# Feed-forward output product as seven products of quarters (Strassen's identity) instead of eight

## The chip, the core and the metric

The kernel runs on one core of a Trainium2 chip. The metric is device time in microseconds from the start of the program to its end, of one launch; lower is better. Before the change it is 849.51 us (median of 3 runs, 849.15 to 849.9). In the text the engines have their names from the profile: PE is TensorE (its matmuls; PEld its weight loads), DVE is VectorE, ACT is ScalarE, POOL is GpSimd, SP is SyncE, which here only issues transfers. SBUF is the on-chip memory of 128 partitions, PSUM the eight banks into which PE writes (128 x 512 float32 each).

## The reference

One layer of a decoder trunk for 512 tokens of 1024 channels, all in float32. The last part is the one that is changed:

```python
hf = rms_norm(x, ffn_norm_g[l]) @ w_ffn_in[l]      # 512x1024 @ 1024x5632
gt, up = jnp.split(hf, 2, axis=-1)                  # 512x2816 each
x = x + (jax.nn.silu(gt) * up) @ w_ffn_out[l]       # 512x2816 @ 2816x1024
```

Ahead of it stand a normed input projection, three branches (an attention without softmax, a convolution of width 31, one of width 3), their gated sum and an output projection; the change doesn't touch them.

## The kernel before, in words

**Precision.** Every float32 operand of a large product is split into two numbers of the type float32r: hi is a cast of the value (ACT, L81), lo the rest (DVE, L82). A product a x b is then three matmuls into the same PSUM bank: a_hi b_hi, a_hi b_lo, a_lo b_hi (mm3, L92 to L95; L90 is the matmul itself). A matmul here has 128 contraction rows, a stationary operand of 128 columns and a moving one of 512.

**Weights.** They come by DMA on SP's queue into one of three buffers `raw` of up to 8 KB a partition (L134), and wsplit turns pieces of up to 1024 columns into a pair `wh`, `wl`, three buffers each. A buffer is loaded or written anew when the last reader of its third predecessor is done, so this ring of three sets how far the transfers and the splits run ahead of PE.

**Order.** PE's instructions stand in the order in which the program writes them. For the other engines a scheduler sets the order when the program is built; the code gives priorities (the loads and splits of weights are high). On the chip each engine works off its row in that order and waits at each instruction for what it needs, so what stands behind a waiting instruction waits too.

**The feed-forward part** runs twice, each time over one half of the 2816 inner channels (11 blocks of 128). ffn_in makes for each block two products of 24 matmuls, gate and up (8 channel blocks x 3 terms, tokens on the moving side), and from them silu(gate) times up, scaled by the reciprocal norm (L759 to L762); the 128 x 512 block h (channels x tokens) is split into hi and lo. Then rows_product makes the output product of this half in two column halves: h is the stationary operand (128 tokens at a time), the weight rows of 512 columns the moving one, and four PSUM banks hold four blocks of 128 tokens. That is 11 x 4 x 3 = 132 matmuls for a column half, 264 for a half of the channels. When a bank is done, DVE adds it to x1, the running sum in SBUF (tiles `v`; L787), and in the second half of the channels into a tile that goes out by DMA from ACT's queue (L790, L791). PSUM tiles: tag mm has four banks, z three, o one.

**POOL** has nothing to do in this part; its last work before it are seven adds for the norm (L717).

Of the kernel before, what the change touches and what calls it, by code (L numbers as in the profile page):

```python
# [14 lines left out]
P = 128  # L15
# [20 lines left out]
def hybrid_layer(ctx, tc, x, mix_norm_g, w_in, q_norm_g, k_norm_g, w_attn_out, conf_dw_w,  # L36
# [19 lines left out]
    BUFS = {"raw": 3, "wh": 3, "wl": 3, "u": 16, "m": 18, "b": 8, "v": 2, "cf": 5, "c": 4, "t": 6,  # L56
            "s": 2, "a": 4, "l0": 2, "r": 2, "l1": 1, "l2": 1, "mm": 4, "z": 3, "o": 1}
    count = [0]
# [684 lines left out]

    half = DFF // P // 2
    later_h = []

    def ffn_in(c, h):
        for j0 in range(0, half, 2):
            n = min(2, half - j0)
            b = (c * half + j0) * P  # L750
            wg, wu = [once(lambda o=o, b=b, n=n: raw(w_ffn_in[:, o + b:o + b + n * P], KT, n * P))
                      for o in (0, DFF)]
            for j in range(n):
                pg = []

                def up(pu, pg=pg):
                    def fn():
                        g, u = tmp(), tmp()
                        nc.vector.tensor_mul(g, pg[0], rstd[0])  # L759
                        act(g, g, AF.Silu)  # L760
                        nc.vector.tensor_mul(u, pu, rstd[0])  # L761
                        nc.vector.tensor_mul(g, g, u)  # L762
                        h.append(split(g, "m" if len(h) < 9 else "b"))
                    if rstd:
# [3 lines left out]

                yield unit(wg, j, lambda: u2, pg.append)
                yield unit(wu, j, lambda: u2, up)  # L770

    for c in range(2):
        h = []
        queue.extend(ffn_in(c, h))
        if c == 0:
# [5 lines left out]
        drain()  # L781
        for n in range(2):
            cs = slice(n * S, (n + 1) * S)

            def add(i, o, n=n, cs=cs, c=c):
                if c == 0:
                    nc.vector.tensor_add(x1[n][:, i, :], o, x1[n][:, i, :])  # L787
                else:
                    y = tmp()
                    nc.vector.tensor_add(y, o, x1[n][:, i, :])  # L790
                    nc.scalar.dma_start(out[i * P:(i + 1) * P, cs], y)  # L791

            queue.append(rows_product(w_ffn_out[c * half * P:(c + 1) * half * P], cs, h, BANKS[n],
                                      add))
            drain()

# [30 lines left out]
```

## Time and profile before

| what | value |
|---|---|
| median of 3 runs | 849.51 us |
| the profiled execution | 849.84 us, its span on the core 848.1 us |
| PE busy | 835.9 us, 99% of the span |
| DVE, ACT, POOL busy | 518.0, 361.8, 35.1 us |
| first half of the output product | 604.9 to 664.8 us |
| second half of the output product | 784.5 to 844.3 us |
| DMA | 81.44 MB, 96 GB/s on average |

A row of the chain of waits gives start, length, engine, tile and line of work that followed without a gap on the way to the end. A row of the groups gives line, engine, operation, output and inputs with shapes, then the number, busy time in all, mean ns of one, and the idle time of the engine ahead of them with what ended it. A row of the timeline gives start and length of one or some instructions in a row. A row of the stretches gives for each engine the busy time and number of instructions (PE, PEld, DVE, ACT, POOL in this order), the granted clock of PE, the DMA engines' share and GB/s. Matmuls overlap, and their ends are modelled, so their pace is read from their starts.

### The profile page before, as it was taken

What the parts mean: (1) busy time and instruction counts of PE and PEld (TensorE: products, weight loads), DVE (VectorE), ACT (ScalarE), POOL (GpSimd) and SP (SyncE); (2) the same over time, 40 slices, a digit from 0 to 9 for tenths busy, and PEclk for the clock granted to TensorE, in tenths of its full rate; (3) what the DMA queues carried; (4) which work ended last, traced back from release to release, by engine and by line L of the source; (5) the groups of instructions that cost most, each with busy time, mean ns of one, the idle gap of its engine ahead of it and who ended that gap; (6) DMA issues with size and microseconds to landing.
All of it is one profiled execution on the core that took longest, in us unless ns stands there. A gap on an engine that the chain in (4) does not pass through costs nothing.

```text
span 848.1 us, 9544 instructions
## 1 busy us (share of the span) xinstructions
PE 835.9 (99%) x3793; PEld 695.6 (82%) x3793; DVE 518.0 (61%) x725; ACT 361.8 (43%) x531; POOL 35.1 (4%) x60
## 2 busy tenths in 40 slices
PE   6999999999999999999999999999999999999998
PEld 6888887888888888888888888888888888888886
DVE  5598799896899999774543455444422544444231
ACT  5436698876664223563342353222221232222120
POOL 2100010002100000000000120000000000000000
PEclk9999999999999999999999999999999999999999
DMA  7333114122112232233253222324224233223311
GB/s 249 103 100 94 56 50 150 50 61 89 50 50 100 73 126 100 71 129 99 100 199 100 64 85 100 100 75 147 72 80 149 100 99 100 75 67 126 102 54 49
DMA packets 73016, 81.44 MB, mean 96 GB/s; under 512 B 1616, under 2 KB 58124, under 8 KB 72972
## 3 DMA queue, kind: packets, MB, share of 16 engines
q1 hardware_dynamic: 71804, 78.74, 28.5%
q10 hardware_dynamic: 1168, 2.10, 0.6%
q8 instruction: 29, 0.48, 0.2%
q14 instruction: 15, 0.12, 0.0%
HBM read 78.74 MB, written 2.10 MB: 95 GB/s over the span
## 4 chain that ended last, share of the span: by engine, by line
PE 95%; DVE 3%; issue 1%; ACT 0%; DMA 0%; SPq 0%; DVEq 0%
PE mm L90 78%; PE z L90 12%; PE o L90 4%; PE mm L296 1%; DVE cf L502 0%; DVE wl L82 0%; DMA m<-in_x_dram 0%; PE z L296 0%; PE mm L705 0%; DVE t L82 0%; DVE m L375 0%; DVE m L376 0%; DVE t L263 0%; DVE s L448 0%; DVE l L82 0%
## 5 line engine op out<-in xcount | busy, mean ns | idle before, releaser
L90 PE MATMUL mm<-u,wh 128*128 128x512 f32 x1536 | 475.1, 390 | 0.0
L90 PEld LDWEIGHTS mm<-u,wh 128*128 128x128 f32 x1536 | 287.4, 188 | 59.4 <-DVE u L710 0.6
L81 ACT CAST wh<-raw 128x1024 fp32r<-128x1024 f32 (+1 forms) x156 | 151.7, 975 | 364.1 <-PE mm L90 260.0
L90 PE MATMUL mm<-u,wl 128*128 128x512 f32 x768 | 299.2, 390 | 0.0
L82 DVE TENSOR_TENSOR wl<-raw,wh 128x1024 fp32r<-128x1024 f32 (+1 forms) x154 | 174.5, 1135 | 122.1 <-ACT wh L81 121.8
L90 PEld LDWEIGHTS mm<-u,wl 128*128 128x128 f32 x768 | 144.2, 188 | 30.0
L502 DVE SCALAR_TENSOR_TENSOR cf<-cf,cols_w,cf 128x512 f32<-128x512 f32 x120 | 89.8, 748 | 3.7 <-ACT cf L500 1.2
L761 DVE TENSOR_TENSOR t<-mm,cf 128x512 f32<-128x512 f32 x22 | 15.2, 691 | 66.8 <-PE mm L90 66.8
L90 PE MATMUL mm<-wh,m 128*128 128x512 f32 x176 | 55.6, 389 | 0.0
L90 PE MATMUL z<-wh,m 128*128 128x512 f32 x132 | 45.2, 392 | 0.0
L759 DVE TENSOR_TENSOR t<-mm,cf 128x512 f32<-128x512 f32 x22 | 15.2, 691 | 42.8 <-PE mm L90 42.8
L90 PE MATMUL mm<-m,wh 128*128 128x512 f32 x128 | 39.4, 389 | 0.0
L90 PEld LDWEIGHTS mm<-wh,m 128*128 128x128 f32 x176 | 33.0, 188 | 6.9
L90 PE MATMUL mm<-wl,m 128*128 128x512 f32 x88 | 34.2, 389 | 0.0
L90 PEld LDWEIGHTS z<-wh,m 128*128 128x128 f32 x132 | 24.8, 188 | 5.1
L90 PEld LDWEIGHTS mm<-m,wh 128*128 128x128 f32 x128 | 24.0, 188 | 4.9
L78 ACT ACTIVATE s<-s 128x384 f32<-128x384 f32 (+1 forms) x48 | 26.9, 560 | 1.1
L90 PE MATMUL z<-wl,m 128*128 128x512 f32 x66 | 25.7, 389 | 0.0
L90 PE MATMUL mm<-m,wl 128*128 128x512 f32 x64 | 24.9, 389 | 0.0
L448 DVE SCALAR_TENSOR_TENSOR s<-z,s 128x384 f32<-128x384 f32 (+1 forms) x24 | 14.4, 598 | 11.6 <-ACT s L78 10.4
L90 PE MATMUL mm<-wh,b 128*128 128x512 f32 x64 | 21.2, 389 | 0.0
L717 POOL TENSOR_TENSOR cf<-cf,t 128x512 f32<-128x512 f32 x7 | 9.9, 1415 | 255.3 <-ACT t L715 255.0
(197 smaller groups left out, 879.9 us busy)
## 6 DMA issues: line engine op xcount, KB each, us to landing
raw<-in_w_in_dram SPq DMA_DIRECT2D x23, 1024.0 KB
raw<-in_w_ffn_in_dram SPq DMA_DIRECT2D x20, 1024.0 KB
raw<-in_w_ffn_out_dram SPq DMA_DIRECT2D x8, 1024.0 KB
raw<-in_w_in_dram SPq DMA_DIRECT2D x10, 512.0 KB
raw<-in_w_o_dram SPq DMA_DIRECT2D x4, 1024.0 KB
raw<-in_w_ffn_out_dram SPq DMA_DIRECT2D x4, 768.0 KB
m<-in_x_dram SPq DMA_DIRECT2D x8, 256.0 KB
raw<-in_w_sc_out_dram SPq DMA_DIRECT2D x2, 1024.0 KB
```

The lines of the kernel that those rows point to most:

```text
L78: table(nc.scalar.activation(o, i, f, **kw))
L81: (copy or nc.scalar.copy)(hi, src)
L82: (sub or nc.vector.tensor_sub)(lo, src, hi.bitcast(F32))
L90: nc.tensor.matmul(o, lhsT, rhs, start=start, stop=stop, skip_group_check=True)
L296: nc.tensor.matmul(pts[f][:, t * P:(t + 1) * P], xblock(xt, t, f), diag, start=True, stop=True, skip_group_check=True)
L448: marks.append(nc.vector.scalar_tensor_tensor(t, z, 0.0, t, ALU.max, ALU.add))
L502: nc.vector.scalar_tensor_tensor(y, pad[:, n:n + S], w(n), y, ALU.mult, ALU.add)
L717: nc.gpsimd.tensor_add(sumsq, sumsq, s)
L759: nc.vector.tensor_mul(g, pg[0], rstd[0])
L761: nc.vector.tensor_mul(u, pu, rstd[0])
```

## The change

The inner channels are taken in two chunks of 12 and 10 blocks instead of 11 and 11, and in pairs of blocks. For a pair, h is a matrix of 2 x 2 quarters A (channel block by half of the tokens, 128 x 256 each) and the weights one of 2 x 2 quarters B (channel block by half of the columns, 128 x 512 each). Instead of eight products of quarters the program makes seven, of sums of quarters (the form of Strassen's identity with 4 + 4 sums ahead and 7 behind; those behind are made on the totals over a chunk, and not for each pair).

- quarters makes four 128 x 256 sums of A per pair on DVE and splits all operands; the operands lie in buffers that earlier parts of the kernel have left (tags m, b, a, l0, l2, s, l1, c).
- ffn_out goes over the pairs twice. Pass 1 makes products 1, 7 and 6 of all pairs (banks p1, p7, p6; 18 matmuls a pair); for it three of the four quarters of weights are loaded, two sums t3, t2 made on DVE (L835, L836) and split. Then p6 and p7 are taken out: ACT copies p1 (L847), DVE adds (L848, L849), POOL makes six adds into x1 (L850 to L852), and p1 goes on in its banks. Pass 2 loads all four quarters, makes t1 and t4 (L863 to L865) and products 2, 3, 4 and 5 (24 matmuls a pair; in the last pair in reverse), 2 into the banks of p1.
- After pass 2, ten adds (L876) bring p5, p4, p3 and p1 into x1, and in the last chunk out.

```diff
@@ -54,7 +54,7 @@
     cst = pool("cst", bufs=1)
     ps = pool("ps", bufs=1, space=PSUM)
     BUFS = {"raw": 3, "wh": 3, "wl": 3, "u": 16, "m": 18, "b": 8, "v": 2, "cf": 5, "c": 4, "t": 6,
-            "s": 2, "a": 4, "l0": 2, "r": 2, "l1": 1, "l2": 1, "mm": 4, "z": 3, "o": 1}
+            "s": 2, "a": 4, "l0": 2, "r": 2, "l1": 1, "l2": 1, "tt": 2, "mm": 4, "z": 3, "o": 1}
     count = [0]
     def alloc(tag, shape=(P, S), dt=F32):
@@ -741,37 +741,156 @@
         defer(16, after)
-    half = DFF // P // 2
-    later_h = []
-
-    def ffn_in(c, h):
-        for j0 in range(0, half, 2):
-            n = min(2, half - j0)
-            b = (c * half + j0) * P
-            wg, wu = [once(lambda o=o, b=b, n=n: raw(w_ffn_in[:, o + b:o + b + n * P], KT, n * P))
+    HT = S // 2
+    SPACE = {2: ["m"] * 9 + ["b"] * 4 + ["a"] * 2 + ["l0"] * 2 + ["l2"],
+             1: ["s"] * 4 + ["l1", "c"]}
+    def operands(space, n):
+        if n == HT:
+            t = alloc(space[1].pop(0), (P, 2, HT), F32R)
+            return t[:, 0], t[:, 1]
+        tag = space[2].pop(0)
+        if tag[0] == "l":
+            t = alloc(tag, (P, 2, n), F32R)
+            return t[:, 0], t[:, 1]
+        return alloc(tag, dt=F32R), alloc(tag, dt=F32R)
+    def quarters(g, space):
+        (a11, a21), (a12, a22) = [[t[:, :HT], t[:, HT:]] for t in g]
+        w1, w2 = tmp(), tmp()
+        s1, s2, s3, s4 = w1[:, :HT], w1[:, HT:], w2[:, :HT], w2[:, HT:]
+        nc.vector.tensor_add(s1, a21, a22)
+        nc.vector.tensor_sub(s2, s1, a11)
+        nc.vector.tensor_sub(s3, a11, a21)
+        nc.vector.tensor_sub(s4, a12, s2)
+        o = []
+        for src in (a11, g[1], w1, w2):
+            n = src.shape[-1]
+            o.append(operands(space, n))
+            split_to(*o[-1], src)
+        cut = lambda k, c: [t[:, c:c + HT] for t in o[k]]
+        return {1: o[0], 2: cut(1, 0), 4: cut(1, HT), 5: cut(2, 0), 6: cut(2, HT), 7: cut(3, 0),
+                3: cut(3, HT)}
+    def ffn_in(j0, n, h, space):
+        for j in range(j0, j0 + n, 2):
+            b = j * P
+            wg, wu = [once(lambda o=o, b=b: raw(w_ffn_in[:, o + b:o + b + 2 * P], KT, 2 * P))
                       for o in (0, DFF)]
-            for j in range(n):
+            gs = []
+            for i in range(2):
                 pg = []
-                def up(pu, pg=pg):
+                def up(pu, pg=pg, gs=gs):
                     def fn():
                         g, u = tmp(), tmp()
                         nc.vector.tensor_mul(g, pg[0], rstd[0])
                         act(g, g, AF.Silu)
                         nc.vector.tensor_mul(u, pu, rstd[0])
                         nc.vector.tensor_mul(g, g, u)
-                        h.append(split(g, "m" if len(h) < 9 else "b"))
+                        gs.append(g)
+                        if len(gs) == 2:
+                            h.append(quarters(gs, space))
                     if rstd:
                         fn()
                     else:
                         defer(9, fn)
-                yield unit(wg, j, lambda: u2, pg.append)
-                yield unit(wu, j, lambda: u2, up)
-
-    for c in range(2):
+                yield unit(wg, i, lambda: u2, pg.append)
+                yield unit(wu, i, lambda: u2, up)
+    def ffn_out(j0, h, last):
+        n = len(h)
+        rows_of = lambda j, k: w_ffn_out[(j0 + 2 * j + k) * P:(j0 + 2 * j + k + 1) * P]
+        def products(j, p, w, banks, start, stop):
+            for i in range(2):
+                a = [t[:, i * P:(i + 1) * P] for t in h[j][p]]
+                mm3(banks[i], a, w, start and j == 0, stop and j == n - 1)
+        def parts(src):
+            hi, lo = wsplit(src)
+            return [(hi[:, i], lo[:, i]) for i in range(src.shape[1])]
+        def sums(fn):
+            with tc.high_priority():
+                t = alloc("tt", (P, 2, S))
+                fn(t[:, 0], t[:, 1])
+            return t
+        p1, p6, p7 = [[psum(tag) for _ in range(2)] for tag in ("mm", "mm", "z")]
+        for j in range(n):
+            with tc.high_priority():
+                w = alloc("raw", (P, 3, S))
+                nc.sync.dma_start(w[:, 0:2], rows_of(j, 0).rearrange("p (n f) -> p n f", n=2))
+                nc.sync.dma_start(w[:, 2], rows_of(j, 1)[:, S:])
+            b11, b12, b22 = [w[:, i] for i in range(3)]
+            def t32(t3, t2):
+                nc.vector.tensor_sub(t3, b22, b12)
+                nc.vector.tensor_add(t2, t3, b11)
+            one, = parts(w[:, 0:1])
+            t3, t2 = parts(sums(t32))
+            products(j, 1, one, p1, True, True)
+            products(j, 7, t3, p7, True, True)
+            products(j, 6, t2, p6, True, True)
+        x = lambda i, c: x1[c][:, i, :]
+        for i in range(2):
+            s1, s2, s3 = tmp(), tmp(), tmp()
+            nc.scalar.copy(s1, p1[i])
+            nc.vector.tensor_add(s2, p6[i], s1)
+            nc.vector.tensor_add(s3, p7[i], s2)
+            nc.gpsimd.tensor_add(x(i, 1), x(i, 1), s2)
+            nc.gpsimd.tensor_add(x(i + 2, 0), x(i + 2, 0), s3)
+            nc.gpsimd.tensor_add(x(i + 2, 1), x(i + 2, 1), s3)
+        p3, p4, p5 = [[psum(tag) for tag in tags] for tags in (("z", "o"), ("mm", "mm"), ("z", "z"))]
+        for j in range(n):
+            with tc.high_priority():
+                w = alloc("raw", (P, 2, 2, S))
+                nc.sync.dma_start(w, w_ffn_out[(j0 + 2 * j) * P:(j0 + 2 * j + 2) * P].rearrange(
+                    "(k p) (n f) -> p k n f", p=P, n=2))
+            (b11, b12), (b21, b22) = [[w[:, k, i] for i in range(2)] for k in range(2)]
+            def t14(t1, t4):
+                v = tmp()
+                nc.vector.tensor_sub(t1, b12, b11)
+                nc.vector.tensor_sub(v, b22, b21)
+                nc.vector.tensor_sub(t4, v, t1)
+            two, three = parts(w[:, 1])
+            t1, t4 = parts(sums(t14))
+            order = [(2, two, p1, False), (3, three, p3, True), (4, t4, p4, True),
+                     (5, t1, p5, True)]
+            for p, part, banks, start in order if j < n - 1 else order[::-1]:
+                products(j, p, part, banks, start, True)
+        def add(i, c, p, final, op=nc.vector.tensor_add):
+            y = tmp() if last and final else x(i, c)
+            op(y, x(i, c), p)
+            if last and final:
+                nc.scalar.dma_start(out[i * P:(i + 1) * P, c * S:(c + 1) * S], y)
+        for i in range(2):
+            add(i, 1, p5[i], False)
+            add(i + 2, 1, p5[i], True)
+        for i in range(2):
+            add(i + 2, 0, p4[i], True, nc.vector.tensor_sub)
+        for i in range(2):
+            add(i, 1, p3[i], True)
+        for i in range(2):
+            add(i, 0, p1[i], True)
+    j0 = 0
+    for c, n in enumerate((12, 10)):
         h = []
-        queue.extend(ffn_in(c, h))
+        queue.extend(ffn_in(j0, n, h, {k: list(v) for k, v in SPACE.items()}))
         if c == 0:
             tick(4)
             for square in [turn(f) for f in range(4, KT)]:
@@ -779,20 +898,8 @@
             tick(1)
             second_norm()
         drain()
-        for n in range(2):
-            cs = slice(n * S, (n + 1) * S)
-
-            def add(i, o, n=n, cs=cs, c=c):
-                if c == 0:
-                    nc.vector.tensor_add(x1[n][:, i, :], o, x1[n][:, i, :])
-                else:
-                    y = tmp()
-                    nc.vector.tensor_add(y, o, x1[n][:, i, :])
-                    nc.scalar.dma_start(out[i * P:(i + 1) * P, cs], y)
-
-            queue.append(rows_product(w_ffn_out[c * half * P:(c + 1) * half * P], cs, h, BANKS[n],
-                                      add))
-            drain()
+        ffn_out(j0, h, c == 1)
+        j0 += n
 _INS = ["x", "mix_norm_g", "w_in", "q_norm_g", "k_norm_g", "w_attn_out", "conf_dw_w", "conf_dw_b",
```

Three places of the order, with tile numbers. DVE where pass 1 meets pass 2 in the first chunk (mm_892_4993 and its neighbour are p6, z_893 and z_894 p7, tt_946 the tile of t1,t4 for the first pair, wl_949 its split, wl_945 that of the second weight rows). Before, at the meeting of the two column halves:

```order
L82 TENSOR_TENSOR wl_877_5024<-raw_875_5021,wh_876_5023 128x1024
L787 TENSOR_TENSOR v_662_3711<-mm_852_4847,v_662_3711 128x512
L787 TENSOR_TENSOR v_662_3711<-mm_853_4848,v_662_3711 128x512
L787 TENSOR_TENSOR v_662_3711<-mm_854_4849,v_662_3711 128x512
L787 TENSOR_TENSOR v_662_3711<-mm_855_4850,v_662_3711 128x512
L82 TENSOR_TENSOR wl_879_5028<-raw_875_5021,wh_878_5027 128x1024
```

and now:

```order
L82 TENSOR_TENSOR wl_945_5215<-raw_943_5212,wh_944_5214 128x1024
L848 TENSOR_TENSOR t_932_5189<-mm_891_4992,t_931_5188 128x512
L849 TENSOR_TENSOR t_933_5190<-z_893_4994,t_932_5189 128x512
L848 TENSOR_TENSOR t_935_5198<-mm_892_4993,t_934_5197 128x512
L849 TENSOR_TENSOR t_936_5199<-z_894_4995,t_935_5198 128x512
L864 TENSOR_TENSOR t_947_5219<-raw_943_5212 128x512
L864 TENSOR_TENSOR t_954_5258<-raw_950_5251 128x512
L864 TENSOR_TENSOR t_961_5297<-raw_957_5290 128x512
L865 TENSOR_TENSOR tt_946_5218<-t_947_5219,tt_946_5218 128x512
L865 TENSOR_TENSOR tt_953_5257<-t_954_5258,tt_953_5257 128x512
L82 TENSOR_TENSOR wl_949_5224<-tt_946_5218,wh_948_5223 128x1024
```

The split that product 4 of the first pair needs stands behind four adds out of PSUM and five sums, two of them for later pairs. POOL's row in the same place, which before was empty:

```order
L717 TENSOR_TENSOR cf_664_3715<-cf_664_3715,t_727_4074 128x512
L850 TENSOR_TENSOR v_663_3713<-v_663_3713,t_932_5189 128x512
L851 TENSOR_TENSOR v_662_3711<-v_662_3711,t_933_5190 128x512
L852 TENSOR_TENSOR v_663_3713<-v_663_3713,t_933_5190 128x512
L850 TENSOR_TENSOR v_663_3713<-v_663_3713,t_935_5198 128x512
L851 TENSOR_TENSOR v_662_3711<-v_662_3711,t_936_5199 128x512
L852 TENSOR_TENSOR v_663_3713<-v_663_3713,t_936_5199 128x512
```

Each of them needs one of DVE's four adds above. DVE where the output product of the first chunk ends and the input product of the second begins. Before (z_871 to o_874 are the banks of the second column half, wl_892 and wl_896 the first two units' weights):

```order
L82 TENSOR_TENSOR wl_892_5190<-raw_890_5187,wh_891_5189 128x1024
L787 TENSOR_TENSOR v_663_3713<-z_871_5017,v_663_3713 128x512
L787 TENSOR_TENSOR v_663_3713<-z_872_5018,v_663_3713 128x512
L787 TENSOR_TENSOR v_663_3713<-z_873_5019,v_663_3713 128x512
L787 TENSOR_TENSOR v_663_3713<-o_874_5020,v_663_3713 128x512
L82 TENSOR_TENSOR wl_896_5221<-raw_894_5218,wh_895_5220 128x1024
```

and now (z_942 is half of p5, mm_939 and mm_940 are p4, mm_889 and mm_890 p1, z_937 and o_938 p3; wl_991 the second unit's weights):

```order
L82 TENSOR_TENSOR wl_991_5490<-raw_989_5487,wh_990_5489 128x1024
L876 TENSOR_TENSOR v_663_3713<-v_663_3713,z_942_5211 128x512
L876 TENSOR_TENSOR v_662_3711<-v_662_3711,mm_939_5208 128x512
L876 TENSOR_TENSOR v_662_3711<-v_662_3711,mm_940_5209 128x512
L82 TENSOR_TENSOR wl_996_5525<-raw_985_5456,wh_995_5524 128x1024
L876 TENSOR_TENSOR v_663_3713<-v_663_3713,z_937_5206 128x512
L876 TENSOR_TENSOR v_663_3713<-v_663_3713,o_938_5207 128x512
L876 TENSOR_TENSOR v_662_3711<-v_662_3711,mm_889_4990 128x512
```

Before, the next input product wrote into banks of tag mm that had been read long ago; now its first bank is that of mm_939, whose add stands behind the split of the second unit's weights. That split's buffer wh_990 is the one that the last pair's t1,t4 had.

## The prediction, made before the changed kernel was run

> **What bounds the kernel now.** I read the page first (busy time, chain of waits), then the chain of waits in order of time and the stretches of the output product, to see whether TensorE ever waits there.
>
> ```profile
> span 848.1 us, 9544 instructions
> PE 835.9 (99%) x3793; PEld 695.6 (82%) x3793; DVE 518.0 (61%) x725; ACT 361.8 (43%) x531; POOL 35.1 (4%) x60
> PE 95%; DVE 3%; issue 1%; ACT 0%; DMA 0%; SPq 0%; DVEq 0%
> ...
> 499.54 135.32 PE mm L90 x597
> ...
> 664.78 149.60 PE mm L90 x660
> ...
> 784.47:844.34 59.87, 59.83 (x264) 49.21 (x263) 17.66 (x21) 10.03 (x11) 0.00 (x0) 1.00 0.19 68
> ```
>
> TensorE makes 95% of the chain, and from 499.5 us to 844.3 us it never waits: one half of the output product is 264 matmuls in 59.87 us, 0.2268 us from one to the next. There every matmul removed is worth 0.2268 us, and every microsecond for which TensorE is made to wait costs one. So the sum is matmuls removed against new waits. The profiled execution took 849.84 us, 0.33 above the median of 849.51.
>
> **What it removes.** Per pair of blocks, eight products of quarters are 48 matmuls (2 blocks x 2 column halves x 4 row blocks x 3 terms), seven are 42. Eleven pairs: 66 fewer, 66 x 0.2268 = **-14.97 us**. The 128x512 form and its operands' layout stay, so I keep the pace.
>
> **What lies beside other work.** Durations, and the pace of DVE when its operations follow each other:
>
> ```profile
> L82 DVE TENSOR_TENSOR wl<-raw,wh 128x1024 fp32r<-128x1024 f32 x126 | 155.2, 1234 | 85.1 <-ACT wh L81 84.8
> L82 DVE TENSOR_TENSOR wl<-raw,wh 128x512 fp32r<-128x512 f32 x28 | 19.3, 688 | 37.1 <-ACT wh L81 37.1
> L81 ACT CAST wh<-raw 128x1024 fp32r<-128x1024 f32 x128 | 134.3, 1052 | 281.1 <-PE mm L90 187.6 <-issue 54.8 <-PE o L90 38.3
> 572.34 0.69 DVE L761 TENSOR_TENSOR t<-mm,cf 128x512 f32<-128x512 f32 x1 [3.31 <-PE mm L90]
> 573.13 0.69 DVE L762 TENSOR_TENSOR t<-t,t 128x512 f32<-128x512 f32 x1
> 573.74 1.22 DVE L82 TENSOR_TENSOR wl<-raw,wh 128x1024 fp32r<-128x1024 f32 x1
> 574.88 0.68 DVE L82 TENSOR_TENSOR m<-t,m 128x512 fp32r<-128x512 f32 x1
> 550.00:600.00 50.00, 50.00 (x222) 41.42 (x221) 23.74 (x29) 15.36 (x19) 0.00 (x0) 1.00 0.32 100
> ```
>
> A 512-wide operation is followed by the next after 0.61 us (573.13 to 573.74), a 1024-wide one after 1.14 us, and one that needs the result just made after 0.79 us (572.34 to 573.13). In the input product DVE is busy 23.7 of 50 us; per pair (96 matmuls, 21.8 us) the change adds four 256-wide sums, one 256-wide and one 512-wide split. A 256-wide one I estimate at 0.42 us from the two rows above, so 5 x 0.42 + 0.69 = 2.8 us, hidden. In pass 1 a pair has 18 matmuls, 4.08 us, against DVE's 3 x 0.61 + 1.14 = 2.97 us; in pass 2, 24 matmuls, 5.44 us, against 3 x 0.61 + 2 x 1.14 = 4.11 us. ACT has less. The loop through the three buffers of split weights, cast 1.05 and subtraction 1.22 and hand-overs, is 2.4 us against 4.08. Laying the rows of the new order one behind another with these times, the narrowest place is pass 1's third pair (DVE still has left-over operand splits there): 0.85 us to spare. I cost all of it at nothing; without that cover, what exceeds the slot is paid eleven times.
>
> The weights of w_ffn_out are now read 1.75 times (0.75 MB per pair in pass 1, 1 MB in pass 2).
>
> ```profile
> 579.95 0.37 SPq L134 DMA_DIRECT2D raw<-in_w_ffn_out_dram  x1
> 580.00:582.00 2.00, 2.00 (x11) 1.65 (x10) 0.00 (x0) 0.00 (x0) 0.00 (x0) 1.00 0.50 49
> 582.00:584.00 2.00, 2.00 (x11) 1.65 (x10) 0.69 (x1) 0.97 (x1) 0.00 (x0) 1.00 1.04 404
> 584.00:586.00 2.00, 2.00 (x11) 1.65 (x10) 1.99 (x3) 0.71 (x2) 0.00 (x0) 1.00 0.19 71
> ```
>
> 1 MB issued at 579.95 is in by about 584.4: 4.4 us. In the new order each tile is issued when the third one before it has been read, some 9.8 us before DVE comes to it. Hidden; SP's queue holds nothing else.
>
> **The seam between the passes, the term that decides.** Call T the moment at which TensorE could start pass 2. Products 2 and 3 of the first pair take it to T+2.72; then product 4 needs the split of t1,t4. In DVE's order that split stands behind the two pairs of adds that take p6 and p7 out of PSUM (L848, L849), and these cannot start before p6's last matmuls are done. So DVE: the adds at T-0.48, +0.31 (needs the one before), +0.92 and +1.71; three subtractions L864 at +2.32, +2.93, +3.54; two more (L865) at +4.15, +4.76; ACT's cast at +4.88 to +5.93; the split's subtraction to +7.2. Product 4's second matmul needs it and would have started at T+2.95: TensorE stands **4.3 us**, if nothing else touches DVE.
>
> Something does. L850 to L852 put six 128x512 adds of SBUF on POOL in just that time, and the trace shows what POOL and DVE do to each other:
>
> ```profile
> 488.69 0.75 DVE L710 SCALAR_TENSOR_TENSOR u<-z,cols,u 128x512 fp32r<-128x512 f32 x1 [0.16 <-ACT u L709]
> 489.59 4.90 POOL L717 TENSOR_TENSOR cf<-cf,t 128x512 f32<-128x512 f32 x3
> 491.17 2.17 DVE L82 TENSOR_TENSOR wl<-raw,wh 128x1024 fp32r<-128x1024 f32 x1 [1.73 <-ACT wh L81]
> L717 POOL TENSOR_TENSOR cf<-cf,t x7: 1283/1292/2160, 468.5 to 492.3; 128x512 f32<-128x512 f32 x7
> ...
> 207.96 1.41 DVE L82 TENSOR_TENSOR wl<-raw,wh 128x1024 fp32r<-128x1024 f32 x1
> 209.30 0.64 DVE L82 TENSOR_TENSOR l<-s,l 128x384 fp32r<-128x384 f32 x1
> 209.86 0.94 DVE L82 TENSOR_TENSOR a<-s,a 128x512 fp32r<-128x512 f32 x1
> ...
> 207.66 0.64 POOL L456 TENSOR_TENSOR r<-s 128x128 f32<-128x128 f32 x1 [14.45 <-DVE s L448]
> 208.36 1.17 POOL L81 CAST l<-r 128x128 fp32r<-128x128 f32 x1
> 209.61 0.65 POOL L82 TENSOR_TENSOR l<-r,l 128x128 fp32r<-128x128 f32 x1
> ```
>
> They take turns, one whole instruction each. POOL's second add of the three ends at 492.25 (1.29 each, 0.08 between); DVE's subtraction, started at 491.17, ends 1.08 later, at 493.34; only then does the third add get on (2.16 instead of 1.29), and it ends 1.15 later. At 207 to 211 the same: DVE ends 1.07 after POOL's 208.30, POOL 0.16 after DVE's 209.37, DVE 0.41 after POOL's 209.53, POOL's last at 210.26 and DVE's 512-wide one 0.54 after that. An operation that reads PSUM is not held (488.69, at 0.75 in the midst of POOL's adds).
>
> So at the seam the four PSUM adds go as above; POOL's first two adds run from +0.25 to +2.91; then it alternates: L864 ends at 3.45, POOL 4.60, L864 5.14, POOL 6.29, L864 6.83, POOL 7.98, L865 8.52, POOL 9.67, L865 10.21, and the split's subtraction at about 11.35 (cast done at 9.6). Product 4's second matmul at 11.4 instead of 2.95: **8.45 us**, twice (each half has its seam): +16.9. The bounds are 4.3 and 8.45 per seam; I take the upper, since all three places where both queue up alternate.
>
> **Does TensorE come back at full pace?** It has then been idle from 2.9 to 9.6, but for one matmul, and till 11.4. The one long idle of the trace:
>
> ```profile
> 7.23 2.08 PE L296 MATMUL mm<-a,m 128*128 128x128 f32 x8 [4.32 <-DVE a L294]
> 9.10 1.49 PE L296 MATMUL z<-a,m 128*128 128x128 f32 x6
> 10.38 0.63 PE L296 MATMUL o<-a,m 128*128 128x128 f32 x2
> 10.81 1.92 PE L296 MATMUL mm<-a,m 128*128 128x128 f32 x8
> ...
> 13.54 1.06 PE L296 MATMUL mm<-a,m 128*128 128x128 f32 x8
> ...
> 15.33 0.83 PE L296 MATMUL mm<-a,m 128*128 128x128 f32 x6
> ```
>
> After 4.32 us of idleness a round of sixteen matmuls takes 3.58 us (7.23 to 10.81), the third one 1.79 (13.54 to 15.33): exactly half pace. The second round, 2.73 us, fits half pace until 12.7, so 5.46 us of it, which loses 2.73 us. The granted clock in the rows reads 1.00 all the while, so it doesn't show this. Bounds: 0 (TensorE was busy before the seam, not fresh) and 2.73 a seam; the seam's gap is longer than 4.32, so I take **2.7, twice: +5.4**. [...]
>
> **Two small terms.** Between the halves, the first matmul of the next input product waits for product 4's bank, whose adds (L876) stand on DVE behind the split of the second unit (1.22), which waits for a weight buffer that product 4 frees 2.56 us before the end: cast to -1.47, split to -0.2, one more add, then the read of that bank to +1.0: **+1.05**. At the end ten adds stand in line 0.61 apart from 4.56 us before TensorE's end, and the last ends 1.62 after it:
>
> ```profile
> 843.91 0.39 PE L90 MATMUL o<-wh,b 128*128 128x512 f32 x1
> 844.34 0.69 DVE L790 TENSOR_TENSOR t<-o,v 128x512 f32<-128x512 f32 x1 [1.35 <-PE o L90]
> ```
>
> Before, it ended at 845.03, 0.89 after 844.14 (843.91 and one pace): **+0.73**, and the last transfer follows as before.
>
> **Sum:** -14.97 + 16.9 + 5.4 + 1.05 + 0.73 = +9.1; 849.84 + 9.1 = 858.9 for a profiled execution, 0.33 less as a median: **858.6 us, slower by 1.1%**.
>
> **Rivals.**
> - *Full pace after the seams* (0.16): no half pace because TensorE had been busy. For it: the half pace was seen only at the kernel's start. Against: the gap is longer than that one. 858.6 - 5.4 = 853.2.
> - *POOL doesn't hold DVE* (0.13), the case on the other side: L864 and L865 go at 0.61, the seam costs 4.3, its gap (3.1 and then 1.3 us) is shorter than 4.32 and brings no half pace. -14.97 + 8.6 + 1.05 + 0.73 = -4.6, so 844.9. The point that decides is 6.6 us a seam, since 2 x 6.6 + 1.78 uses up 14.97. Against it stand the rows at 207 and 491.
> - *Seams near that point* (0.05): some adds of POOL fall into DVE's waits: 848 to 851.
> - *The seam is covered after all* (0.04): the split is ready in time; -14.97 + 1.78, so 836.3.
> - *DVE becomes the bound in the passes* (0.08): the 0.85 us of slack are not there, and each of the 22 slots is 0.25 us long: +5.5, so 864.1. DVE's 61% speak against it, its in-order queue for it.
>
> The forecast itself has 0.54, with 856 to 861.5 (the half pace's loss a third smaller or larger, since one case gives no spread, and 0.4 a seam). Within 0.2% (1.7 us, what a measurement of this kernel can tell from no change) lies the fourth line, 0.05; faster are 0.13 + 0.04 = 0.17; slower 0.54 + 0.16 + 0.08 = 0.78. The range 849.5 to 864 leaves out the faster ones and half of the last, about 0.2.
>
> **What would show it.** In the changed profile: 66 matmuls fewer; TensorE at 0.2268 in both passes; in the middle of each output product a gap of some 6.7 us, one matmul, and another gap of 1.7, released by DVE's wl<-tt; L864 and L865 at 1.5 us or more while POOL's adds run, at 0.69 after; behind the gap matmuls some 0.43 apart for 3 to 7 us; a wait of 1 us before the next input product. Wrong would be a gap of 4 us, short L864 rows, or waits for wl at other pairs.

## The result and the profile after

The changed kernel takes 858.17 us (median of 4 executions, 857.73 to 858.86) against 849.58 us (849.15 to 849.9) for the kernel before: ratio 1.0102, 95% interval 1.0085 to 1.012, slower by 1.0%. The forecast was 858.6 us. The profiled execution took 858.28 us.

The page of the changed kernel: span, busy time, granted clock in 40 slices, shares of the chain of waits.

```profile
span 856.2 us, 9698 instructions
PE 826.7 (97%) x3727; PEld 685.4 (80%) x3727; DVE 612.6 (72%) x878; ACT 393.0 (46%) x577; POOL 53.5 (6%) x72
PEclk9999999999999999999999999999997999999979
PE 91%; DVE 6%; issue 1%; ACT 1%; DMA 1%; SPq 0%; DVEq 0%
```

There are 66 matmuls fewer (3793 to 3727), and still the span is 8.1 us longer. DVE's share of the chain went from 3% to 6%. The clock's row has two dips at slices 31 and 39; the page of before had none. What TensorE waited for from the output product on (in total, number of times, longest; the other rows of this view lie ahead of it):

```profile
PE mm L90 <- ACT wh L81: 13.5, 2, 6.8
PE mm L90 <- DVE wl L82: 1.8, 2, 0.9
PE mm L90 <- DVE v L876: 1.0, 1, 1.0
```

These waits stand at three places: the two seams between pass 1 and pass 2, and the boundary between the chunks. No row names a wait inside a pass. The timeline of the first seam, for DVE, POOL, ACT and TensorE (start, length, instruction; in brackets the idle time before it and what ended it):

```profile
638.55 0.69 DVE L848 TENSOR_TENSOR t<-mm,t 128x512 f32<-128x512 f32 x1 [1.21 <-PE mm L90]
...
640.60 0.69 DVE L849 TENSOR_TENSOR t<-z,t 128x512 f32<-128x512 f32 x1
641.21 4.55 DVE L864 TENSOR_TENSOR t<-raw 128x512 f32<-128x512 f32 x3
645.68 3.42 DVE L865 TENSOR_TENSOR tt<-t,tt 128x512 f32<-128x512 f32 x2
649.02 1.21 DVE L82 TENSOR_TENSOR wl<-tt,wh 128x1024 fp32r<-128x1024 f32 x1
...
640.59 1.29 POOL L851 TENSOR_TENSOR v<-v,t 128x512 f32<-128x512 f32 x1
641.83 1.71 POOL L852 TENSOR_TENSOR v<-v,t 128x512 f32<-128x512 f32 x1
...
647.52 1.04 ACT L81 CAST wh<-tt 128x1024 fp32r<-128x1024 f32 x1 [10.46 <-DVE tt L865]
...
641.46 0.39 PE L90 MATMUL o<-wh,m 128*128 128x512 f32 x1
648.61 0.79 PE L90 MATMUL mm<-wh,m 128*128 128x512 f32 x1 [6.77 <-ACT wh L81]
650.29 0.80 PE L90 MATMUL mm<-wl,m 128*128 128x512 f32 x1 [0.89 <-DVE wl L82]
...
655.09 0.40 PE L90 MATMUL mm<-wh,m 128*128 128x512 f32 x1
```

The five subtractions of L864 and L865 take 7.8 us (641.21 to 649.02), 1.56 each, and POOL's adds 1.7 instead of 1.3, for as long as both engines have such work. Product 4's second matmul should have started two slots after product 3's last (641.46), at 641.91; it starts at 650.29, so TensorE stands 8.38 us, and 8.37 at the second seam. From there eleven matmuls take 4.80 us (650.29 to 655.09) where 2.50 are due: 2.30 us lost to half pace. At the second seam it is twelve in 5.17 us, 2.45 lost. The stretches around it show the granted clock (the number behind POOL's):

```profile
644.50:645.00 0.50, 0.00 (x0) 0.00 (x0) 0.50 (x1) 0.00 (x0) 0.50 (x1) 0.76 0.91 360
645.00:654.50 9.50, 5.00 (x11) 3.63 (x12) 9.50 (x10) 2.94 (x3) 3.55 (x3) 0.50 0.38 139
654.50:655.00 0.50, 0.50 (x2) 0.40 (x2) 0.41 (x1) 0.00 (x0) 0.00 (x0) 0.51 1.01 418
```

A mean of 0.76 over 644.5 to 645.0 puts the fall from 1.00 to 0.50 at 644.76, 2.9 us after TensorE's last work; 0.51 over 654.5 to 655.0 puts the return at 654.99, 10.23 us later. At the second seam, by means of 0.83 over 818.5 to 819.0 and 0.93 over 829.0 to 829.5, half clock runs from 818.83 to 829.07, 10.24 us, and it begins 174.07 us after the first.

The boundary between the chunks and the tail:

```profile
682.10 0.39 PE L90 MATMUL mm<-wh,l 128*128 128x512 f32 x1
683.46 0.70 PE L90 MATMUL mm<-u,wh 128*128 128x512 f32 x2 [0.98 <-DVE v L876]
...
850.59 0.39 PE L90 MATMUL mm<-wh,b 128*128 128x512 f32 x1
...
851.05 1.28 DVE L876 TENSOR_TENSOR t<-v,mm 128x512 f32<-128x512 f32 x2
...
850.00:852.00 2.00, 0.98 (x5) 0.48 (x3) 2.00 (x4) 0.00 (x0) 0.00 (x0) 1.00 1.06 408
852.00:854.00 2.00, 0.00 (x0) 0.00 (x0) 0.33 (x1) 0.00 (x0) 0.00 (x0) 0.74 1.06 405
```

At the boundary the next matmul comes 1.36 us after the last, 1.13 late. From the last matmul to the end of the span it is 5.61 us against 4.19 before, 1.42 more; eight output tiles now leave together, and the DMA engines are full (share 1.06) for 4 us.

The sum of what the trace shows: -14.97 + 8.38 + 8.37 + 2.30 + 2.45 + 1.13 + 1.42 = +9.1. This execution reached the long stretch of matmuls ahead of the output product 1.2 us earlier (498.32 against 499.54), so +7.9 is to be compared with the span's +8.1; 0.2 us is not placed. Nothing ahead of that stretch was changed, and in the traces of the runs below it begins anywhere between 498.1 and 499.65; a difference of a microsecond between two runs can come from there.

### The profile page after: what moved, and what is told of

Same layout as the page of the kernel before. It is cut to its first block, busy times and chain, and to the rows that moved or that the text cites. A ratio compares the mean times of both kernels' runs of the same rounds, so it can differ in the third digit from the quotient of the medians.

```text
span 856.2 us, 9698 instructions
## 1 busy us (share of the span) xinstructions
PE 826.7 (97%) x3727; PEld 685.4 (80%) x3727; DVE 612.6 (72%) x878; ACT 393.0 (46%) x577; POOL 53.5 (6%) x72
## 4 chain that ended last, share of the span: by engine, by line
PE 91%; DVE 6%; issue 1%; ACT 1%; DMA 1%; SPq 0%; DVEq 0%
PE mm L90 76%; PE z L90 11%; PE o L90 3%; DVE t L864 1%; DVE wl L82 1%; DVE tt L865 1%; DMA m<-in_x_dram 1%; DVE cf L502 0%; DVE t L876 0%; PE mm L705 0%; DVE t L848 0%; DVE v L876 0%; ACT wh L81 0%; DVE t L283 0%; DVE t L82 0%
## 5 line engine op out<-in xcount | busy, mean ns | idle before, releaser
L81 ACT CAST wh<-raw 128x1024 fp32r<-128x1024 f32 (+1 forms) x154 | 147.0, 955 | 286.8 <-PE mm L90 230.8
L82 DVE TENSOR_TENSOR wl<-raw,wh 128x1024 fp32r<-128x1024 f32 (+1 forms) x152 | 168.6, 1109 | 66.3 <-ACT wh L81 65.8
L90 PE MATMUL mm<-wh,m 128*128 128x512 f32 x104 | 37.4, 412 | 13.5 <-ACT wh L81 13.5
L81 ACT CAST wh<-tt 128x1024 fp32r<-128x1024 f32 x22 | 23.1, 1052 | 44.4 <-DVE tt L865 20.9
L90 PEld LDWEIGHTS mm<-wh,m 128*128 128x128 f32 x104 | 20.9, 201 | 18.7 <-ACT wh L81 14.4
L82 DVE TENSOR_TENSOR wl<-tt,wh 128x1024 fp32r<-128x1024 f32 x22 | 26.9, 1222 | 10.0 <-ACT wh L81 9.9
L90 PE MATMUL z<-wh,m 128*128 128x512 f32 x84 | 31.5, 415 | 0.0
L850 POOL TENSOR_TENSOR v<-v,t 128x512 f32<-128x512 f32 x4 | 6.0, 1502 | 310.6 <-DVE t L848 310.6
L90 PE MATMUL mm<-wh,b 128*128 128x512 f32 x72 | 23.9, 389 | 0.0
L90 PE MATMUL mm<-wl,m 128*128 128x512 f32 x52 | 21.5, 414 | 1.8 <-DVE wl L82 1.8
```

Of the source, the lines that this page charges most:

```text
L81: (copy or nc.scalar.copy)(hi, src)
L82: (sub or nc.vector.tensor_sub)(lo, src, hi.bitcast(F32))
L90: nc.tensor.matmul(o, lhsT, rhs, start=start, stop=stop, skip_group_check=True)
L850: nc.gpsimd.tensor_add(x(i, 1), x(i, 1), s2)
```

## The experiments

All times are medians; every ratio is to the kernel before, run on the same chip beside it. The edits are to the changed kernel, except where said.

| run | edit | us | ratio, 95% interval |
|---|---|---|---|
| the change | | 858.17 | 1.0102, 1.0085 to 1.012 |
| r1_own_v | another buffer for v | 846.38 | 0.9964, 0.995 to 0.9978 |
| r2_no_pool_adds | without POOL's six adds | 850.2 | 1.0008, 0.9999 to 1.0017 |
| r3_fill30 | 30 matmuls in the gap | 854.75 | 1.0063, 1.0048 to 1.0078 |
| r4_chunks_only | eight products, chunks of 12 and 10 | 849.58 | 1.0001, 0.9991 to 1.001 |
| r7_four_adds | four of the six adds | 855.21 | 1.0062, 1.0046 to 1.0077 |
| r8_fill18 | 18 matmuls in the gap | 858.56 | 1.0108, 1.0092 to 1.0125 |
| r9_fill24 | 24 matmuls in the gap | 856.2 | 1.0074, 1.0057 to 1.0091 |
| r6_reordered_pool | seam in another order | 842.91 | 0.9917, 0.9903 to 0.9932 |
| r10_reordered_no_end | and POOL's adds on DVE, later | 837.43 | 0.9854, 0.984 to 0.9869 |
| r5_reordered | and product 4 first at the end | 835.6 | 0.9832, 0.9817 to 0.9846 |

### Is it the chunks?

In the kernel before:

```diff
-    half = DFF // P // 2
+    SIZES = (12, 10)
...
-        for j0 in range(0, half, 2):
-            n = min(2, half - j0)
-            b = (c * half + j0) * P
+        for j0 in range(0, SIZES[c], 2):
+            n = 2
+            b = (c * SIZES[0] + j0) * P
```

> The kernel before, with eight products, but in chunks of 12 and 10 blocks instead of 11 and 11. Theory (the cost is all in the new seams): the chunks alone change nothing, 849.6 us within 0.5. Rival (the uneven chunks cost something by themselves, in the operands' buffers or at the boundary): 850.5 to 852, and the saving of seven products would then have been larger than I reckon.

849.58 us, within 0.1% of the kernel before. The chunks cost nothing; the whole difference is the seven products.

### Is it POOL?

```diff
-            nc.gpsimd.tensor_add(x(i, 1), x(i, 1), s2)
-            nc.gpsimd.tensor_add(x(i + 2, 0), x(i + 2, 0), s3)
-            nc.gpsimd.tensor_add(x(i + 2, 1), x(i + 2, 1), s3)
```

> POOL's six adds of each seam (L850 to L852) are left out, so the second chunk of rows and columns lacks products 1, 6 and 7 there; DVE's order stays as it is. Theory (POOL and DVE take turns): L864 and L865 now follow each other at 0.61 us, the wait before product 4's second matmul shrinks from 8.4 to 4.3 us a seam, in two pieces (3.1 and 1.3). If so short a gap brings no half pace, 858.2 - 2 x 4.1 - 2 x 2.3 = 845.4; if it does, 850. Rival (L864 and L865 are slow for another reason, the landing of the weights for instance): they stay at 1.5 us and the time stays at 858.

The first seam without the adds (three lines are gone, so L861 is L864 and L862 is L865), DVE, then TensorE, then two stretches:

```profile
641.27 1.88 DVE L861 TENSOR_TENSOR t<-raw 128x512 f32<-128x512 f32 x3
643.07 1.29 DVE L862 TENSOR_TENSOR tt<-t,tt 128x512 f32<-128x512 f32 x2
...
641.51 0.39 PE L90 MATMUL o<-wh,m 128*128 128x512 f32 x1
644.94 0.50 PE L90 MATMUL mm<-wh,m 128*128 128x512 f32 x1 [3.04 <-ACT wh L81]
646.20 0.80 PE L90 MATMUL mm<-wl,m 128*128 128x512 f32 x1 [0.76 <-DVE wl L82]
...
645.00:652.00 7.00, 6.24 (x15) 4.67 (x16) 5.82 (x7) 2.48 (x3) 0.00 (x0) 0.52 0.58 219
...
816.00:819.00 3.00, 2.56 (x6) 2.07 (x7) 3.00 (x5) 1.02 (x2) 0.00 (x0) 0.50 0.42 85
```

The five go at 0.61 each, and the stall to product 4's second matmul is 646.20 - 641.96 = 4.24 us instead of 8.38: POOL's six adds cost 4.1 us a seam, as the prediction laid it out instruction by instruction. The rival cause, slow reads while weights land, is out. But the time is 850.2 and not 845.4: the two short gaps (3.04 and 0.76) brought half pace too, for about 7 us at the first seam (13 matmuls in 5.71 us, 2.76 lost) and 3.4 at the second (1.5 lost). The clock falls at 645.31 and at 815.97, 170.66 us apart, and comes back after 6.83 and 3.42 us (means of 0.81 over 645.0 to 645.5, 0.86 over 652.0 to 652.5, 0.97 over 815.5 to 816.0, 0.61 over 819.0 to 819.5). The ten executions range from 849.3 to 851.6 at mean clocks of 0.991 to 0.994.

With four of the six adds (L852 taken out):

> As the change, without L852, so four adds of POOL at each seam instead of six; the lower right part of the result lacks products 6 and 7. Theory (turn by turn: each further add of POOL that is queued holds DVE once): DVE is held twice instead of four times, 4.24 + 2 x 1.03 = 6.3 us to product 4's second matmul instead of 8.4, 858.2 - 2 x 2.1 = 854.0 us, three of L864's and L865's five rows still near 0.6. Rival (POOL slows all that DVE does while it runs, in proportion): the five are stretched alike, and the stall is 4.24 + 4/6 x 4.14 = 7.0, 855.5.

The first seam, where L863 is L864 and L864 is L865:

```profile
642.50 4.55 DVE L863 TENSOR_TENSOR t<-raw 128x512 f32<-128x512 f32 x3
646.97 1.28 DVE L864 TENSOR_TENSOR tt<-t,tt 128x512 f32<-128x512 f32 x2
...
643.12 1.71 POOL L850 TENSOR_TENSOR v<-v,t 128x512 f32<-128x512 f32 x1
644.79 1.71 POOL L851 TENSOR_TENSOR v<-v,t 128x512 f32<-128x512 f32 x1
```

855.21 us, nearer to the rival's 855.5, but the rows decide, and they speak for turns. I had miscounted: three operations are held, not two, since POOL's second add is still under way when the first of them starts. The three are stretched exactly as with six adds (4.55), and the two behind POOL's last add not at all (1.28). That is turn by turn; stretching in proportion would have touched all five. The two adds that are left out save 1.48 us a seam, 2.96 in all. That the medians differ by just as much is chance: in the profiled executions half pace also costs 0.9 us less than in the change (1.26 and 2.56 us), and the long stretch begins 1.3 us later. With work queued on both sides DVE and POOL alternate in this trace, one whole instruction each: 1.52 us for each of the three subtractions, 1.71 for each of POOL's last two adds, and 0.64 for each of the two subtractions behind them.

### Is the half pace a matter of idleness?

TensorE gets more matmuls of the same form in the gap, into a bank that is started afresh later:

```diff
+                if j == 0 and p == 4:
+                    for _ in range(30):
+                        mm(p5[0], h[0][3][0][:, 0:P], two[0], True, True)
                 products(j, p, part, banks, start, True)
```

> Before product 4 of the first pair of each second pass TensorE gets 30 more matmuls of the same form (6.8 us), into a bank that product 5 starts afresh later, so that it works while it would wait; the splits that it waits for don't change. Theory (half pace follows idleness): the matmuls behind the seam go at 0.227, and 2 x 2.3 us are saved: 853.6 us. Rival (they are slow for what they read, or for what DVE and ACT do at that time): they stay at 0.43 and the time at 858.2 or above. If the 30 delay product 4 itself, the stall to its second matmul is longer than 8.4 us in the trace, and the time is read against that.

```profile
643.01 6.96 PE L90 MATMUL z<-wh,m 128*128 128x512 f32 x30
650.04 0.49 PE L90 MATMUL mm<-wh,m 128*128 128x512 f32 x1
651.74 0.50 PE L90 MATMUL mm<-wl,m 128*128 128x512 f32 x1 [1.21 <-DVE wl L82]
...
640.00:660.00 20.00, 18.73 (x81) 14.96 (x81) 19.54 (x20) 5.05 (x5) 9.35 (x6) 1.00 0.30 105
```

The clock stays at 1.00 and the matmuls behind the seam go at 0.23. The median fell by 3.4 us, not by the expected 4.6. Counted from the slot in which product 4 would start, so without the part of the program ahead of it, which took 1.3 us longer in this execution, it is 847.64 - 643.01 = 204.63 us to the last matmul, against 850.59 - 641.69 = 208.90: 4.3 us, nearly all of the 2.30 + 2.45 that half pace had cost. Work whose result is thrown away saved time here.

How much idleness it takes, with 18 and 24 instead of 30:

> As the run with 30 more matmuls, but 18 of them (4.1 us), so that TensorE idles 2.7 us before product 4's first matmul and about 1.4 before its second. Theory (half pace follows a stretch of some 3.4 us with next to no work, as 3.0 + 0.8 us with one matmul between gave it without POOL's adds): half pace again, 856.5 to 858.5, mean clock below 1 in every execution. Rival (it needs one unbroken idle stretch of about 3 us): none, 854.7 as with 30, clock 1.00.

> As the runs with 30 and 18 more matmuls, now 24 (5.4 us), so that TensorE idles about 1.4 us before product 4's first matmul and about 1.2 before its second, 2.6 us in all; with 18 it was 2.75 and 1.18, and half pace came. Theory (half pace needs a stretch of 3.4 us with next to no work): none now, clock 1.00, and the time is that with 30, 854.7 us. Rival (each idle microsecond of the seam brings its share of half pace): between the two, 856 to 857, clock below 1.

With 18, half pace came at both seams (1.55 and 1.72 us lost in the profiled execution), and the time is 858.56 us, just above the expected range: the rival that asks for one unbroken gap of 3 us is out. With 24, in the profiled execution, TensorE idles 1.42 and 1.18 us at both seams, and the first seam has no half pace while the second has it:

```profile
650.00:656.00 6.00, 5.04 (x22) 4.22 (x23) 5.93 (x8) 2.18 (x3) 0.00 (x0) 1.00 0.44 160
820.93 0.50 PE L90 MATMUL mm<-wh,m 128*128 128x512 f32 x1 [1.42 <-ACT wh L81]
822.60 0.50 PE L90 MATMUL mm<-wl,m 128*128 128x512 f32 x1 [1.18 <-DVE wl L82]
...
822.50:823.00 0.50, 0.40 (x2) 0.35 (x3) 0.50 (x2) 0.27 (x1) 0.00 (x0) 1.00 0.00 0
823.00:826.50 3.50, 3.50 (x11) 2.70 (x10) 3.50 (x5) 0.00 (x0) 0.00 (x0) 0.54 0.44 140
826.50:827.00 0.50, 0.50 (x3) 0.46 (x2) 0.47 (x2) 0.00 (x0) 0.00 (x0) 0.79 1.01 418
```

The same gaps, two outcomes, within one execution; the four executions took 854.9 us at mean clock 1.000, 855.9 and 856.7 at 0.998, 856.49 at 0.996. Neither expectation was right as it stood. By the means of 0.54 and 0.79 the clock is halved from 823.3 to 826.7, for 3.41 us. Half clock lasted 10.23 and 10.24 us in the change, 6.83 and 3.42 in r2, 3.42 at both seams of r8 (651.04 to 654.46 and 825.12 to 828.54): one, two or three times 3.41. A fixed grid of windows of 10.23 / 3 = 3.41 us, my estimate from these lengths, would explain the two outcomes. At the second seam half clock is then one window; the window ahead of it runs from 819.9 to 823.3 and holds 2.2 us of idleness (1.04 before the matmul at 820.93, and 1.18). Counted back by fifty windows, the grid has an edge at about 649.2 at the first seam, which parts the idleness: 1.4 us ahead of the edge, 1.2 behind it. By this estimate a window two thirds idle lost the clock, and one 40% idle didn't. That half pace needs a stretch of 3.4 us with next to no work, as both theories assumed, no run shows.

The other traces fit the same estimate, though none was run to test it. The two falls of the clock lie 174.07 us apart in the change, 170.66 in r2 and 174.08 in r8, which is 51, 50 and 51 times 3.413; in r7 the two returns to full pace, read from the starts of the matmuls (652.60 and 826.62), lie 51 times 3.413 apart. On this grid the nine windows that lost the clock (two each in the change, r2, r7 and r8, one in r9; in r7 they are placed by the two returns and the mean clock of 0.988) held 2.0 to 3.2 us of idleness, and no window of the output product that kept it held more than 1.7. At half clock, a window with at most 0.47 us of idleness brought the full clock back, and one with 0.74 or more didn't. By this estimate, then, a window needn't be idle throughout to cost the clock; where between 1.7 and 2.0 us the limit lies isn't measured.

### Is it the order, and why does the split stand so late?

In the change, v of t14 takes one of the six `t` buffers. The drains s1, s2, s3 for two row blocks, written ahead of it, take all six, so L864 of the very first pair must wait for a drain to be over. One word undoes it:

```diff
-                v = tmp()
+                v = alloc("cf")
```

> One buffer changed: the difference v of t14 no longer takes one of the six t buffers, which the drains of p6 and p7 occupy, but a free cf buffer. In the new order of DVE the split of t1,t4 of the first pair stands ahead of the first drain (L848). Theory (the seam is an order: the split stands behind the drains, and POOL's adds stretch what stands between): the 8.4 us before product 4's second matmul go, and with them the matmuls at half pace (2.3 us a seam). What is late next is the second L848, which now stands behind the split of the second pair: I lay it at 5.6 us after the pass could begin, against 3.4 at which its bank is wanted, so about 2.3 us a seam, too short for half pace. 858.2 - 2 x (8.4 + 2.3) + 2 x 2.3 = 841.5 us (839 to 845), the first of these runs that is faster than before. Rival (DVE has too much to do around the seam, whatever the order): the wait only moves to the splits of the second pair, 5 us or more a seam, 850 to 858.

```profile
PE mm L90 <- DVE wl L82: 2.6, 2, 1.5
PE mm L90 <- DVE t L848: 2.4, 2, 1.6
PE mm L90 <- ACT t L847: 1.9, 2, 0.9
```

846.38 us: faster than the kernel before, by this edit alone. The 8.4 us and the half pace are gone (mean clock 0.998 to 1.0). The time lies above the expected 839 to 845 us, since the cost that is left is larger than I had laid out. The second L848 is late, as expected (1.6 us), but the second copy of p1 (L847) is late as well (0.9, behind a cast on ACT), and so are splits of a later pair (1.1 and 1.5, L82), because POOL's adds now hold the second and third pair's sums and splits (1.78 us for a sum and 2.30 for a split, instead of 0.68 and 1.22). That is 6.9 us in these rows where I reckoned 4.6. By the starts of TensorE's matmuls it is more: from the first of the long stretch to the last of the kernel it takes 339.70 us (499.30 to 839.00), 10.25 more than in r5_reordered below, and all but the boundary's 1.26 of that is the seams'.

The next three take the rest away step by step. The first of them (the sums of the third pair are put behind the drains in the same way as the second pair's split):

```diff
-            products(j, 7, t3, p7, True, True)
-            products(j, 6, t2, p6, True, True)
+            for p, part, banks in ((7, t3, p7), (6, t2, p6))[::1 if j < n - 1 else -1]:
+                products(j, p, part, banks, True, True)
...
+        s = [[tmp() for _ in range(3)] for _ in range(2)]
         for i in range(2):
-            s1, s2, s3 = tmp(), tmp(), tmp()
-            nc.scalar.copy(s1, p1[i])
-            nc.vector.tensor_add(s2, p6[i], s1)
-            nc.vector.tensor_add(s3, p7[i], s2)
+            nc.scalar.copy(s[i][0], p1[i])
+            nc.vector.tensor_add(s[i][1], p6[i], s[i][0])
+        for i in range(2):
+            s1, s2, s3 = s[i]
+            behind = nc.vector.tensor_add(s3, p7[i], s2).ins
...
+            if j == 1:
+                queued_after[nsplit[0] + 1] = [behind]
...
-                v = tmp()
+                v = alloc("cf")
```

> Of the same kernel only the order of the seam (v in cf, products 1, 6, 7 in the last pair, drains of p6 then p7 ahead of the second pair's split); POOL's six adds stay at the seam, and so does the end of the output product. Theory (POOL's adds cost even behind a good order, since they hold the second pair's split and sums): product 4 no longer waits, but the second and third pair's splits come 1 to 1.5 us late each, 2 to 3 us a seam: 836 + 1.1 + 2 x 2.5 = 842 us (839.5 to 844). Rival (POOL's adds matter only when the first pair's split is behind them): no wait but the boundary's, 837.1.

842.91 us, as the theory had it. TensorE no longer waits at product 4 of the first pair; it waits at product 4 of the pairs behind it, up to 0.9 us at a time. DVE at the first seam shows what POOL still holds (L869 and L870 are sums of a later pair, in the change L863 and L864):

```profile
641.01 1.46 DVE L869 TENSOR_TENSOR tt<-raw 128x512 f32<-128x512 f32 x1
642.39 2.31 DVE L82 TENSOR_TENSOR wl<-raw,wh 128x1024 fp32r<-128x1024 f32 x1
644.63 1.77 DVE L870 TENSOR_TENSOR cf<-raw 128x512 f32<-128x512 f32 x1
646.33 2.31 DVE L82 TENSOR_TENSOR wl<-tt,wh 128x1024 fp32r<-128x1024 f32 x1
```

Then the six adds go from POOL to DVE, two behind the splits of each of the third, fourth and fifth pair, where DVE has time:

```diff
-            nc.gpsimd.tensor_add(x(i, 1), x(i, 1), s2)
-            nc.gpsimd.tensor_add(x(i + 2, 0), x(i + 2, 0), s3)
-            nc.gpsimd.tensor_add(x(i + 2, 1), x(i + 2, 1), s3)
...
+            if 1 < j < 5:
+                for k in (2 * j - 4, 2 * j - 3):
+                    i, y = k // 3, k % 3
+                    o = x(i, 1) if y == 0 else x(i + 2, y - 1)
+                    with tc.issue_after(split_last[0]):
+                        nc.vector.tensor_add(o, o, s[i][2 if y else 1])
```

> As the reordered kernel, but with the end of each output product as in the change: product 5 first, then 4, and product 4's adds behind the split of the next weights. Theory (the boundary and the longer tail are separate terms): the wait of about 1.1 us for product 4's bank comes back between the halves and the tail stays, 835.6 + 1.1 = 836.7 us. Rival (with DVE less loaded there, the bank comes free in time anyhow): 835.6.

837.43 us, 5.5 less than with the adds on POOL: even in a good order POOL's adds cost 2.7 us a seam. TensorE's one wait in the output product is that at the boundary (1.0 us behind L887, the change's L876), so the rival is out. Last, product 4 comes first in the last pair, and its adds stand ahead of the next weight splits:

```diff
-            for p, part, banks, start in order if j < n - 1 else order[::-1]:
+            if j == n - 1:
+                order = [order[k] for k in (2, 3, 1, 0)]
+            for p, part, banks, start in order:
...
         for i in range(2):
+            ins = add(i + 2, 0, p4[i], True, nc.vector.tensor_sub)
+        if not last:
+            queued_after[nsplit[0] + 1] = queued_after[nsplit[0] + 2] = [ins]
+        for i in range(2):
             add(i, 1, p5[i], False)
             add(i + 2, 1, p5[i], True)
-        for i in range(2):
-            add(i + 2, 0, p4[i], True, nc.vector.tensor_sub)
```

> All causes found so far are taken away together, with the same seven products. v takes a cf buffer, so that the split of t1,t4 of the first pair stands ahead of the drains; the last pair of pass 1 multiplies in the order 1, 6, 7; both drains of p6 come first, then both of p7, and the second pair's split only behind them; the six adds of SBUF go from POOL to DVE, two in each of the pairs 3 to 5; at the end of the pass product 4 comes first and its adds stand ahead of the next weight splits. Theory (order and POOL are the whole loss): no seam, no wait at the boundary, 849.58 - 14.97 + 1.4 for the tail = 836.0 us; at most 838.5, since two adds more make 5.3 us of DVE work in a slot of 5.44. Rival (seven products cost TensorE something that I have not seen, in the passes or from DVE's greater load): 841 or more, with waits that lie at other pairs.

835.6 us, 1.7% faster than the kernel before, where 836.0 was expected. The page's span, and all that TensorE still waited for in the whole program:

```profile
span 833.2 us, 9688 instructions
PE mm L298 <- DVE a L296: 3.8, 1, 3.8
PE o L231 <- POOL big_ident L222: 2.6, 1, 2.6
PE mm L92 <- DVE t L84: 1.4, 2, 1.1
```

None of the three lies in the output product. The median is 1.8 us below the run before it. TensorE is 1.26 us quicker from the last matmul of product 3 of the first seam's pair to the very last (186.32 us against 187.58), a little over the expected 1.1; the rest is no more than the part ahead of the output product varies by. The tail stays at 833.2 - 827.56 = 5.6 us.

## Why the prediction was right, and where it was not

- **Matmuls removed, -14.97.** Right. With all waits taken away (r5_reordered) TensorE needs 329.45 us (498.11 to 827.56) from the first matmul of the long stretch to the last of the kernel, against 344.37 before (499.54 to 843.91): 14.92 less, so the seven products bring what they should. The passes keep 0.2268, and neither DVE nor the weights bound them, so the rival with DVE as the bound (864.1) is out.
- **The seams, 2 x 8.45.** Right in size (8.38 and 8.37) and in cause. Both bounds were met: 4.24 without POOL's adds, 8.38 with six. The prediction took the place of the split behind the drains from the order; the runs showed the reason, the buffer of v, and that this one choice is worth 11.8 us (858.17 to 846.38).
- **Half pace, 2 x 2.7.** Right in kind, too large in size: 2.30 and 2.45. The step that mis-sized it took the second round at the kernel's start for the price. By the estimate of a 3.41 us grid, what is lost runs from product 4's second matmul to the end of the first busy window, and depends on where the grid lies; in the runs it was 1.3 to 2.8 us a seam. The rival of full pace (853.2) is out.
- **Boundary, 1.05.** Right: 1.13.
- **Tail, 0.73.** Mis-sized: 1.42. DVE's last add ends about 1.5 us after TensorE, near the 1.62 of the working, which accounts for 0.62; but "the last transfer follows as before" was wrong: eight transfers now leave together and fill the DMA engines for 4 us, and from the last add to the end it is 3.87 us instead of 3.07. No run separates this; it is read from the rows.
- The two misses cancel: the loss to half pace is 0.65 us smaller than forecast, the tail 0.69 longer. That the total is within 0.1% owes something to this, and to chance, since the part ahead of the output product varies by more than that.
- **A rival priced wrongly.** "POOL doesn't hold DVE" was put at 844.9, a clear gain, because a gap of 3.1 and then 1.3 us "brings no half pace". Measured without POOL's adds: 850.2, no gain at all. The point that was said to decide the sign, 6.6 us a seam, was set too high for the same reason: with 4.24 us of stall a seam the change already only breaks even.

## What to carry to other kernels

Before an edit that takes PSUM banks out in the middle of a product, look at what the next work on the draining engine needs, down to the buffer tags: one temporary from a full ring put a split behind the drains and cost 12 us, and a word mended it. Keep GpSimd's adds off stretches in which VectorE feeds TensorE: here VectorE's subtractions took 1.56 us each beside them instead of 0.61, and the same adds on VectorE itself, in its idle slots, were 5.5 us cheaper. Idleness of TensorE can cost more than itself: here 2.0 us or more within a window of some 3.4 us (by the estimate above) brought another 1.3 to 2.8 us of half pace a seam, and if such a gap can't be closed, work that is thrown away inside it can pay (3.4 us here).

## What was not expected of the hardware

- The clock was lost on far less idleness than the 4.32 us that the prediction took as its measure, and by the estimate of the grid what counts is the idleness within one window: 3.04 + 0.76 us with a matmul between in r2_no_pool_adds, 2.75 + 1.18 in r8_fill18, and 1.42 + 1.18 at one seam of r9_fill24 but not at the other. Single gaps of 1.0 to 1.6 us (r1_own_v) left it at 0.998 to 1.0 on average.
- The same program can thus differ from one execution to the next: r2_no_pool_adds from 849.3 to 851.6 us (mean clock 0.994 and 0.991), r9_fill24 from 854.9 to 856.7 (1.000 and 0.998).
- Here the granted clock did show the half pace (0.50), while at the kernel's start, with matmuls at the same half pace (a round of sixteen in 3.58 us, later in 1.79), it read 1.00; whether the same thing slowed them there isn't shown.
